# Four of eight pairs with seven products in the down projection of a decoder block

## The chip, the cores and the metric

The kernel runs on one core of a Trainium2 chip. The metric is the device time of one execution in microseconds. The kernel before took 1487.53 us (median of 3 runs, 1486.21 to 1487.73). One further execution was taken with the hardware profiler and took 1486.3 us; every row below comes from that one. The profiler granted TensorE a clock of 0.997 of full speed over it, which is the 2.4 GHz level throughout.

## The reference: what is computed

One block of a decoder for 256 tokens of 2048 channels in float32:

```
h = rmsnorm(x);  z = h @ w_in    # 2048 -> 3072 for three mixers, 512 q, 576 kv, 4 * 2048 gates
y_i = mixer_i(z) @ proj_i                # pooling, convolution, spatial gating, latent attention
x = x + rmsnorm((sum of sigmoid(gate_i) * y_i) @ w_out)
h = rmsnorm(x)
f = square(relu(h @ w_up)) @ w_down      # 2048 -> 8192 -> 2048
x = x + rmsnorm(f)
```

## The kernel before

Every product of float32 matrices is made of three TensorE matmuls, on a high and a low part of each operand (xh·wh, xh·wl, xl·wh). A weight item of 1 MB comes by a DMA on SP's queue into one of three `raw` buffers. ACT rounds a piece of it into `hi` (L102), DVE subtracts that from it into `lo` (L103). `hi` and `lo` have four buffers each, and `w_get` keeps three pieces ahead of TensorE, so that a cast waits until TensorE has read the piece four places before it.

PSUM has eight banks of 512 columns, four of a kind `bank` and four `aux`; a matrix product holds its bank from its first matmul until ACT or DVE has read it. The order of the work is the order in which Python code emits it: generators (`spawn`, `yield`, `tick`) put the small work of norms, rotary embedding and convolution between the pieces of the large products, and a scheduler keeps each engine's order fixed. An instruction that waits therefore holds back all that stands behind it on its engine.

**The start.** The inputs are loaded in pairs of 128 channels together with the weights of q and of kv. The first weights of q come by a DMA that ACT issues (L174) behind one for the gains. Sixteen such steps accumulate `zq` (two banks of 512 columns) and `zkv` (two of 288); the second half of kv, 224 + 64 columns, follows in a loop of its own. When it ends, the statistic of the input norm is ready, and `latent` copies `zq` and `zkv` to SBUF with the scale (L365), takes squares (L369), normalises (L375), transposes (`tp`) and splits into `lat` (L381). TensorE goes on with the convolution's blocks `cva` and `cvg`, which take over the banks of `zkv`. Where a generator needs a product of TensorE, that product stands between those blocks (`rb_ps`, `tp`).

**Norms.** The sum of squares of a row arrives by ACT's accumulator in four parts; `total` adds them, and `rsqrt` takes the power -0.5 on POOL (L263) and refines it on DVE with one Newton step (L265 to L270). The first of these norms over rows is in the middle, between the output projection and the up projection (`first_norm`, `hn_part`); the last one is at the end, in the tail.

**The up and down projections** run in four quarters, q = 0 to 3. A quarter computes 16 blocks of 128 hidden channels (`block_tr`, L223 and L226), keeps them split in `fx`, and multiplies them by its rows of w_down. All of that but the last quarter's second half goes through `eight_sums`: seven calls, for q = 0, 1, 2 with column halves h = 0 and 1, and q = 3 with h = 0. It handles 16 k-blocks as eight pairs of 2 x 2 blocks. A pair listed in `SEVEN` uses a Strassen scheme: seven products of 128x512 into banks M1 to M7, from weights that DVE has combined in place (`first`, `second`, L159 to L163) and activations that `keep_sums` prepared in `sx`. Any other pair uses the eight plain products, into M2, M3, M4 and M8. Eight banks are summed over all pairs; at the end they are added to `acc`, in SBUF. For q = 0 ACT copies them (L1169), for q = 1 to 3 DVE adds them (L1171). `combine` then adds the eight sums to the four results (L1118), once per column half. The last quarter's second half uses plain products, `chunk_nat` for columns c = 2, and a group for each token tile for c = 3.

**The tail.** While that runs, `xr`, the residual kept in DRAM, is loaded back by POOL (L1184), and `combine(0)` runs on DVE with ACT's squares (L1141). Then come `evac_f` for the last columns (L1190), the norm, and `put` (L1213), which multiplies, adds the residual and starts a DMA of 256 KB to the output for each of eight pieces.

Of the kernel before, what the change touches and what calls it, by code (L numbers as in the profile page):

```python
# [15 lines left out]
P = 128  # L16
# [16 lines left out]
QK_SCALE = 192 ** -0.5  # L33
TWO_PI = 6.283185307179586

SEVEN = (1, 3, 5)
SEVEN_G = (1, 3, 5)


# [35 lines left out]
def trunk(ctx: ExitStack, tc: tile.TileContext, t: dict):  # L75
# [90 lines left out]
    def w_emit():  # L166
        if not pending:
            it = next(items, None)
            if it is None:
                return False  # L170
            src, n, step = it
            raw = wp.tile([P, PC], F32, tag="raw", name="raw", bufs=3)
            if step == "first":
                nc.scalar.dma_start(raw[:, :512], src[0][:, :512])  # L174
                nc.sync.dma_start(raw[:, HC:n], src[1])
                nc.sync.dma_start(raw[:, 512:HC], src[0][:, 512:])
                pending.extend((raw[:, o:o + m], None) for o, m in ((0, 512), (HC, 288), (512, 512), (HC + 288, 288)))
# [79 lines left out]
    mhalf = cst.tile([P, NT], F32, name="mhalf")  # L257
    G.memset(mhalf, -0.5)

    def rsqrt(out, var, n):  # L260

        u = w1("nw")[:, :n]
        G.tensor_tensor(out, var, mhalf[:, :n], ALU.pow)  # L263
        if n == 1:
            V.scalar_tensor_tensor(u, out, var, out, ALU.mult, ALU.mult)  # L265
        else:
            V.tensor_tensor(u, out, out, ALU.mult)
            V.tensor_tensor(u, u, var, ALU.mult)
        V.tensor_scalar(u, u, -0.5, 1.5, ALU.mult, ALU.add)
        V.tensor_tensor(out, out, u, ALU.mult)  # L270
# [6 lines left out]
            o += w  # L277

    g_in = small("g_in", KD)
    nc.scalar.dma_start(g_in, t["pre_mix_g"])  # L280
    warm = small("warm", NT)
    A.activation(warm, mhalf, AF.Copy, scale=mhalf[:, :1])
    hx = big.tile([P, KD, NT, S], F32R, tag="A", name="hx")
    xT = big.tile([P, KD, S], F32, tag="B", name="xT")
    ones = cst.tile([P, P], F32, name="ones")
    V.memset(ones, 1.0 / 512)

# [20 lines left out]
    zq = [aux(f"zq{i}") for i in range(NT)]  # L308
    zkv = [[bank(f"zkv{i}{c}") for c in range(2)] for i in range(NT)]
    for k in range(0, KD, 2):  # L310
        nc.sync.dma_start(xT[:, k:k + 2], t["xT"][:, k:k + 2])
        for j in range(k, k + 2):
            if k == 0 or j == k:
                w = [w_get(0), w_get(0)]
            A.activation(hx[:, j, 0], xT[:, j], AF.Copy, scale=g_in[:, j:j + 1])
            V.scalar_tensor_tensor(hx[:, j, 1], xT[:, j], g_in[:, j:j + 1], hx[:, j, 0].bitcast(F32),
                                   ALU.mult, ALU.subtract)
            r = j - k if k else 0
            mm_nat(zq, hx, j, w[0], r * 512, 512, j == 0, j == KD - 1)
# [35 lines left out]
    lat = x16("lat")  # L355
    cqx, ckvx = lat[:, :4], lat[:, 4:]

    def latent(zs, xs, gain, name):

        cn = t4("cn")  # L360
        st = small(f"st_{name}", NT)
        for i in range(NT):
            o = i * 512
            for ps, w in zs[i]:
                A.activation(cn[:, o:o + w], ps[:, :w], AF.Copy, scale=rstd[:, i:i + 1])  # L365
                o += w
# [20 lines left out]
    def spread(out, v):  # L387

        for i in range(NT):
            V.tensor_scalar(out[:, i * P:(i + 1) * P], ident, 0.0, v[:, i:i + 1], ALU.mult, ALU.add)  # L390

    def setup():
        for k in range(KD - 6, KD, 2):
            add_square(k)
# [7 lines left out]
        V.tensor_scalar(ss, ps[:, :NT], 512.0 / D, EPS, ALU.mult, ALU.add)  # L402
        rsqrt(rstd, ss, NT)
        yield 0
        spawn(latent([[(zq[i], 512)] for i in range(NT)], cqx, qg, "cq"))
        yield 0

        posf = small("posf", NT)
# [62 lines left out]
        done.add("kr")  # L471

    spawn(rope_key())
    spawn(latent([[(zkv[i][0], 288), (zkv[i][1], 224)] for i in range(NT)], ckvx, kvg, "ckv"))


    glu = t4("glu").rearrange("p (b s) -> p b s", b=4)
# [467 lines left out]
    def total(parts, n, name):  # L945
# [4 lines left out]

        def rest(beside=None):
            o = small(name)
            v = V.scalar_tensor_tensor(pre, parts[:, n - 1:n], 1.0 / D, pre, ALU.mult, ALU.add)
            if beside:
                with tc.issue_after(v.ins):
                    beside()
            rsqrt(o, pre, 1)
            return o
        return rest

# [126 lines left out]
    def first_hidden(fx):  # L1087
# [17 lines left out]
            yield 1  # L1105
        done.add("u0")

    dr = ctx.enter_context(tc.tile_pool(name="dr", bufs=1, space=bass.MemoryType.DRAM))
    kept = dr.tile([P, NT, D], F32, name="kept")
    xr = mp.tile([P, NT, D], F32, tag="og", name="xr")  # L1110
    sx = mp.tile([P, len(SEVEN), 2, 512], F32R, tag="xg", name="sx")
    fst = [small(f"fst{i}", 4) for i in range(NT)]
    acc = [None, None]

    def combine(h, final):

# [22 lines left out]

    def square_f(i, c, *_):  # L1140
        A.activation(w2("sq"), row_at(i, c), AF.Square, scale=r2sq[i], accum_out=fst[i][:, c:c + 1])  # L1141

    for q in range(NQ):
        fx = big.tile([P, KQ, 2, S], F32R, tag="B", name="fx")
# [22 lines left out]
        def evac(h, b, ps):  # L1167
            if q == 0:
                A.copy(acc[h][:, b], ps[b])  # L1169
            else:  # L1170
                V.tensor_tensor(acc[h][:, b], ps[b], acc[h][:, b], ALU.add)  # L1171

        for h in range(2 if q < NQ - 1 else 1):
            eight_sums(fx, lambda i, o: tuple(sx[:, i, a, o * P:(o + 1) * P] for a in range(2)), SEVEN,
# [33 lines left out]
    rest = [total(fst[i], 4, f"rf{i}") for i in range(NT)]  # L1208
    ws = [w_get(0) for _ in range(4)]

    def put(i, r, c):
# [99 lines left out]
```

## Time and profile before

| what | value |
|---|---|
| median of 3 runs | 1487.53 us |
| profiled execution, whole | 1486.3 us |
| its span, first to last instruction | 1484.6 us |
| PE busy | 1469.7 us, 99% |
| DVE busy | 1171.1 us, 79% |
| ACT busy | 791.5 us, 53% |
| POOL busy | 19.3 us, 1% |
| DMA, 40 slices | 0.3 to 0.8 busy, mean 199 GB/s |

The busy time of an engine is a mean over stages. The chain of waits, followed back from the last instruction, says which engine's work set the end; a list by engine says what that engine waited for and how long. The rows of a timeline begin with the start in microseconds from the span's start and a busy time; what stands in brackets is the idle time of the engine just before the row, and what ended it.

### The profile page before, as it was taken

To read this page: it belongs to the slowest core of one execution; us is meant where nothing else is said; L and a number is where in the kernel's file an instruction comes from. 1 tells how busy PE (TensorE), PEld (TensorE's weight loads), DVE (VectorE), ACT (ScalarE), POOL (GpSimd) and SP (SyncE) were. 2 spreads that over 40 slices of the span, in tenths; PEclk is the share of its full clock that TensorE was granted. 3 is DMA by queue.
4 is the path that set the end of the run, shared out by engine and by line. 5 is a ranking of instruction groups with operands and counts; after the bars stand their busy time and mean duration, and the time that the engine had idled before them with its cause. 6 is when DMAs were issued, how large, how long until landed. Compare 5 with 4: busy or idle time off the path is not lost.

```text
span 1484.6 us, 18697 instructions
## 1 busy us (share of the span) xinstructions
PE 1469.7 (99%) x7213; PEld 1242.1 (84%) x7213; DVE 1171.1 (79%) x1644; ACT 791.5 (53%) x1062; POOL 19.3 (1%) x36
## 2 busy tenths in 40 slices
PE   9999999999999999999999999999999999999997
PEld 8888888888888888888888888888888888888885
DVE  6878788977888888887657877767887779887785
ACT  6655656445554554554444756655544555555552
POOL 0100000000000000000000000000000000000000
PEclk9999999999999999999999999999999999999998
DMA  8555544545645645646756656555566546555573
GB/s 287 206 193 173 182 158 161 198 171 170 226 170 200 225 170 200 225 168 231 284 201 227 253 170 211 216 197 184 172 211 217 184 166 227 204 193 189 167 270 111
DMA packets 57688, 295.75 MB, mean 199 GB/s; under 512 B 5184, under 2 KB 5312, under 8 KB 37120
## 3 DMA queue, kind: packets, MB, share of 16 engines
q1 hardware_dynamic: 55360, 280.41, 53.9%
q0 software_dynamic: 1952, 13.89, 2.5%
q8 instruction: 56, 0.92, 0.2%
q10 hardware_dynamic: 288, 0.27, 0.1%
q14 instruction: 32, 0.26, 0.0%
HBM read 290.36 MB, written 4.19 MB: 198 GB/s over the span
## 4 chain that ended last, share of the span: by engine, by line
PE 96%; DMA 2%; issue 1%; DVE 1%; ACT 0%; POOL 0%; POOLq 0%; DVEq 0%; ACTq 0%
PE up L223 15%; PE sum L814 12%; PE sum L813 12%; PE sum L815 12%; PE up L226 8%; PE yb L212 2%; PE yb L213 2%; PE yb L214 2%; PE zg L212 2%; PE zg L214 2%; PE zg L213 2%; PE o L213 1%; PE o L214 1%; PE o L212 1%; DMA xg<-in_x 1%; PE hd L223 1%
## 5 line engine op out<-in xcount | busy, mean ns | idle before, releaser
L102 ACT CAST hi<-raw 128x1024 fp32r<-128x1024 f32 (+2 forms) x612 | 614.3, 1015 | 453.3 <-PE sum L815 144.8
L103 DVE TENSOR_TENSOR lo<-raw,hi 128x1024 fp32r<-128x1024 f32 (+2 forms) x612 | 708.4, 1175 | 181.3 <-ACT hi L102 173.8
L223 PE MATMUL up<-h,hi 128*128 128x512 f32 x960 | 229.9, 391 | 0.0
L223 PEld LDWEIGHTS up<-h,hi 128*128 128x128 f32 x960 | 176.4, 188 | 34.1
L814 PE MATMUL sum<-lo,fx 128*128 128x512 f32 x343 | 133.4, 389 | 0.0
L813 PE MATMUL sum<-hi,fx 128*128 128x512 f32 x343 | 133.4, 389 | 0.0
L815 PE MATMUL sum<-hi,fx 128*128 128x512 f32 x343 | 133.4, 389 | 0.0
L226 PEld LDWEIGHTS up<-h,lo 128*128 128x128 f32 x960 | 123.1, 191 | 4.7
L226 PE MATMUL up<-h,lo 128*128 128x256 f32 x960 | 124.8, 283 | 0.0
L814 PE MATMUL sum<-lo,hx 128*128 128x512 f32 x312 | 121.4, 389 | 0.0
L815 PE MATMUL sum<-hi,hx 128*128 128x512 f32 x312 | 121.4, 389 | 0.0
L813 PE MATMUL sum<-hi,hx 128*128 128x512 f32 x312 | 121.4, 389 | 0.0
L251 ACT COPY jn<-up 128x256 f32<-128x256 f32 x60 | 22.3, 372 | 122.9 <-PE up L223 122.8
L252 DVE TENSOR_TENSOR u<-up,jn 128x256 f32<-128x256 f32 x60 | 25.4, 423 | 71.5 <-ACT jn L251 71.5
L813 PEld LDWEIGHTS sum<-hi,fx 128*128 128x128 f32 x343 | 64.4, 188 | 13.6
L815 PEld LDWEIGHTS sum<-hi,fx 128*128 128x128 f32 x343 | 64.4, 188 | 13.4
L814 PEld LDWEIGHTS sum<-lo,fx 128*128 128x128 f32 x343 | 64.4, 188 | 13.4
L814 PEld LDWEIGHTS sum<-lo,hx 128*128 128x128 f32 x312 | 58.6, 188 | 12.3
L813 PEld LDWEIGHTS sum<-hi,hx 128*128 128x128 f32 x312 | 58.6, 188 | 12.2
L815 PEld LDWEIGHTS sum<-hi,hx 128*128 128x128 f32 x312 | 58.6, 188 | 12.2
L505 DVE SCALAR_TENSOR_TENSOR cy<-glu,consts,cy 128x253 f32<-128x253 f32 (+15 forms) x120 | 55.2, 462 | 0.6
L212 PE MATMUL zg<-hi,hx 128*128 128x512 f32 x128 | 51.5, 403 | 0.0
(409 smaller groups left out, 2327.8 us busy)
## 6 DMA issues: line engine op xcount, KB each, us to landing
raw<-in_w_g SPq DMA_DIRECT2D x64, 1024.0 KB, 5.4
raw<-in_w_up SPq DMA_DIRECT2D x64, 1024.0 KB, 4.9
raw<-in_w_down SPq DMA_DIRECT2D x64, 1024.0 KB, 5.5
raw<-in_w_out SPq DMA_DIRECT2D x16, 1024.0 KB, 4.9
raw<-in_attn_proj SPq DMA_DIRECT2D x8, 1024.0 KB, 4.9
raw<-in_w_ca SPq DMA_DIRECT2D x4, 1024.0 KB, 4.9
raw<-in_w_cg SPq DMA_DIRECT2D x4, 1024.0 KB, 4.9
raw<-in_w_sv SPq DMA_DIRECT2D x4, 1024.0 KB, 4.8
```

The costliest lines, as they stand in the source:

```text
L102: a = A.copy(hi, src)
L103: return a, V.tensor_tensor(lo, src, hi.bitcast(F32), ALU.subtract)
L212: T.matmul(o, xh, wh, start=first, stop=False)
L213: T.matmul(o, xh, wl, start=False, stop=False)
L214: T.matmul(o, xl, wh, start=False, stop=last)
L223: T.matmul(ps, w[0][:, off:off + P], xs[:, k].rearrange("p a s -> p (a s)"), start=first, stop=last)
L226: T.matmul(ps[:, :S], w[1][:, off:off + P], xs[:, k, 0], start=False, stop=False)
L252: V.tensor_tensor(out, ps[:, :S], r, ALU.add)
L505: V.scalar_tensor_tensor(y, glu[:, b, :S - w], c, y, ALU.mult, ALU.add)
L813: T.matmul(ps[b], xh, wh, start=first, stop=False)
L814: T.matmul(ps[b], xh, wl, start=False, stop=False)
L815: T.matmul(ps[b], xl, wh, start=False, stop=not left[b])
```

## The change

- `SEVEN` goes from (1, 3, 5) to (0, 2, 4, 6): four pairs have seven products, four have eight. `sx` gets four entries, and the first block of the hidden layer keeps sums for pair 0.
- For q = 1 to 3 the eight bank sums are no longer added to `acc` by DVE. ACT copies each bank into a buffer (four into a new `stage`, four into work tiles `e`), and POOL issues a DMA of 256 KB that adds the buffer to `acc`.
- `combine` begins 4 steps later for h = 0 and 6 for h = 1.
- First loads: the first weights of q go on SP's queue as its first item, and the first inputs come in two DMAs, one on ACT's queue and one on SP's.
- `latent` is taken apart: the first 288 columns of `zkv` are copied in `setup`, with `zq`, before the rest.
- The norms over rows take a square root on ACT and a reciprocal on DVE, where POOL's power stood; a square root of a dummy is emitted ahead of the output projection.
- In the tail, the last eight k-blocks of the last token tile are cut: four as before with 512 columns, and four twice with 256 columns, into two new banks `end0` and `end1`, with their own squares and gains; the norm of that tile then adds five parts.

```
-SEVEN = (1, 3, 5)
+SEVEN = (0, 2, 4, 6)
...
             if step == "first":
-                nc.scalar.dma_start(raw[:, :512], src[0][:, :512])
+                nc.sync.dma_start(raw[:, :512], src[0][:, :512])
+                nc.sync.dma_start(xT[:, 1:2], t["xT"][:, 1:2])
...
-        G.tensor_tensor(out, var, mhalf[:, :n], ALU.pow)
+        if root is None:
+            G.tensor_tensor(out, var, mhalf[:, :n], ALU.pow)
+        else:
+            V.reciprocal(out, root)
...
+    nc.scalar.dma_start(xT[:, :1], t["xT"][:, :1])
+    nc.scalar.dma_start(g_in, t["pre_mix_g"])
...
-        spawn(latent([[(zq[i], 512)] for i in range(NT)], cqx, qg, "cq"))
+        spawn(latent([[(zq[i], 0, 512)] for i in range(NT)], cqx, qg, "cq"))
+        half.append(part_of([[(zkv[i][0], 0, 288)] for i in range(NT)]))
...
-    spawn(latent([[(zkv[i][0], 288), (zkv[i][1], 224)] for i in range(NT)], ckvx, kvg, "ckv"))
+    spawn(latent([[(zkv[i][1], 288, 224)] for i in range(NT)], ckvx, kvg, "ckv", half[0]))
...
+            root = small(name + "s")
+            A.activation(root, parts[:, n - 1:n], AF.Sqrt, scale=1.0 / D, bias=pre)
...
-            rsqrt(o, pre, 1)
+            rsqrt(o, var, 1, root)
...
+    stage = mp.tile([P, PC], F32, tag="rg", name="stage", bufs=2)
...
+        yield 6 if h else 4
         add(M2, M1)
...
-                V.tensor_tensor(acc[h][:, b], ps[b], acc[h][:, b], ALU.add)
+                e = stage[:, b * 512:(b + 1) * 512] if b < 4 else w2("e")
+                A.copy(e, ps[b])
+                G.dma_start(acc[h][:, b], e, accum_op=ALU.add)
...
-    tok_group(ps[1], fx, 8, 1, ws, False, True)
-    with tc.issue_after(evac_f(1, 3).ins):
-        put(0, ra, 3)
-    rb = rest[1](lambda: gain_f(1, 3))
+    tok_group(ps[1], fx, 8, 1, ws[:2], False, True)
+    f = row_at(1, 3)
+    V.tensor_tensor(f, ps[1], f, ALU.add)
+    ends = [bank(f"end{h}") for h in range(2)]
+    for h in range(2):
+        for j in range(4):
+            mm_tok(ends[h][:, :S], fx, 12 + j, 1, ws[2 + j // 2], j % 2 * 512 + h * S, S, j == 0, j == 3)
```

Three places where the order of instructions moves are shown below.

Before:

```order
L426 ACT_TABLE_LOAD
L426 ACTIVATE sin<-ang 128x64
L102 CAST hi<-raw 128x1024
L427 ACTIVATE cos<-rnd 128x64
L381 ACTIVATE lat<-tp,consts 128x256 x2
L365 ACTIVATE cn<-zkv_97,rstd 128x224
L369 ACTIVATE sq,st_ckv<-cn 128x512
L381 ACTIVATE lat<-tp,consts 128x256
L365 ACTIVATE cn<-zkv_99,rstd 128x224
L102 CAST hi<-raw 128x1024
```

ACT at the same place with the change:

```order
L438 ACT_TABLE_LOAD
L438 ACTIVATE sin<-ang 128x64
L102 CAST hi<-raw 128x1024
L439 ACTIVATE cos<-rnd 128x64
L102 CAST hi<-raw 128x1024
L390 ACTIVATE lat<-tp,consts 128x256 x2
L102 CAST hi<-raw 128x1024
L369 ACTIVATE cn<-zkv_98,rstd 128x224
L390 ACTIVATE lat<-tp,consts 128x256
L369 ACTIVATE cn<-zkv_100,rstd 128x224
```

The copies of the second kv columns now stand behind two more casts of weights.

POOL in the last quarter; `acc_7439` holds the first column half, and the eight DMAs into it are, in order, for M1 and M7, then M5 and M6, then M2, M4, M3 and M8. Before:

```order
L1080 DMA kept<-xr 128x4096
L263 TENSOR_TENSOR r_7048<-r20p,mhalf 128x1
L263 TENSOR_TENSOR r_7171<-r21p,mhalf 128x1
L1184 DMA xr<-kept 128x4096
L263 TENSOR_TENSOR rf_12353<-rf0p,mhalf 128x1
L263 TENSOR_TENSOR rf_12396<-rf1p,mhalf 128x1
```

POOL with the change:

```order
L1199 DMA acc_7440<-stage 128x512 x4
L1199 DMA acc_7440<-e 128x512 x4
L1199 DMA acc_7439<-stage 128x512 x2
L1212 DMA xr<-kept 128x4096
L1199 DMA acc_7439<-stage 128x512 x2
L1199 DMA acc_7439<-e 128x512 x4
```

The load of the residual now stands between the second and the third of the last eight adding DMAs.

DVE at the combination of the first column half, beside the end of the last `eight_sums` and the columns c = 2. Before:

```order
L1118 TENSOR_TENSOR acc_7417<-acc_7417 128x512
L103 TENSOR_TENSOR lo<-raw,hi 128x1024
L1171 TENSOR_TENSOR acc_7417<-sum,acc_7417 128x512 x2
L103 TENSOR_TENSOR lo<-raw,hi 128x1024
L1118 TENSOR_TENSOR acc_7417<-acc_7417 128x512
L1180 SCALAR_TENSOR_TENSOR acc_7417<-acc_7417,r2sq_6699,rg 128x512
L1118 TENSOR_TENSOR acc_7417<-acc_7417 128x512
L103 TENSOR_TENSOR lo<-raw,hi 128x1024
L1118 TENSOR_TENSOR acc_7417<-acc_7417 128x512 x3
```

DVE with the change:

```order
L163 TENSOR_TENSOR raw<-raw 128x512
L103 TENSOR_TENSOR lo<-raw,hi 128x1024 x9
L1135 TENSOR_TENSOR acc_7439<-acc_7439 128x512 x2
L103 TENSOR_TENSOR lo<-raw,hi 128x1024
L1135 TENSOR_TENSOR acc_7439<-acc_7439 128x512
L1208 SCALAR_TENSOR_TENSOR acc_7439<-acc_7439,r2sq_6707,rg 128x512
L1135 TENSOR_TENSOR acc_7439<-acc_7439 128x512
L103 TENSOR_TENSOR lo<-raw,hi 128x1024
L1135 TENSOR_TENSOR acc_7439<-acc_7439 128x512 x3
```

The first two additions of the combination now stand behind nine `lo` (four of the last two pairs, five of the columns c = 2) and ahead of the sixth `lo` of c = 2.

## Rows read from the trace of the kernel before

**Rows 1.** The page: busy time of TensorE, and the chain's shares by engine.
```profile
PE 1469.7 (99%) x7213; PEld 1242.1 (84%) x7213; DVE 1171.1 (79%) x1644; ACT 791.5 (53%) x1062; POOL 19.3 (1%) x36
PE 96%; DMA 2%; issue 1%; DVE 1%; ACT 0%; POOL 0%; POOLq 0%; DVEq 0%; ACTq 0%
```

**Rows 2.** Waits of TensorE: line, releaser, us in total, times, longest.
```profile
PE zq L212 <- ACT hi L102: 1.6, 1, 1.6
PE cva L223 <- ACT cn L365: 1.1, 1, 1.1
PE tph L1019 <- DVE hn L1014: 0.2, 1, 0.2
```

**Rows 3.** Timeline of TensorE in `eight_sums`, first and last of 45 matmuls: start, us.
```profile
1239.84 0.39 PE L813 MATMUL sum<-hi,fx 128*128 128x512 f32 x1
...
1249.84 0.39 PE L815 MATMUL sum<-hi,fx 128*128 128x512 f32 x1
```

**Rows 4.** Timeline of the start, ACT and TensorE.
```profile
6.55 0.62 ACT L102 CAST hi<-raw 128x512 fp32r<-128x512 f32 x1 [1.30 <-DMA raw<-in_w_q]
...
13.57 1.62 ACT L102 CAST hi<-raw 128x1024 fp32r<-128x1024 f32 x2 [0.66 <-DMA raw<-in_w_q]
...
16.04 0.39 PE L212 MATMUL zq<-hi,hx 128*128 128x512 f32 x1
```

**Rows 5.** Windows, 0 to 25 us; last three columns: PE clock, DMA share, GB/s.
```profile
0.00:25.00 25.00, 22.26 (x118) 19.98 (x119) 15.79 (x27) 17.00 (x30) 1.19 (x8) 1.00 0.91 316
```

**Rows 6.** Timelines of ACT, DVE and TensorE around the latents, 56 to 71 us.
```profile
57.87 1.28 ACT L426 ACT_TABLE_LOAD   x1
59.74 0.87 DVE L375 TENSOR_SCALAR cn<-cn,r_cq 128x512 f32<-128x512 f32 x2
62.89 0.45 ACT L365 ACTIVATE cn<-zkv,rstd 128x224 f32<-128x224 f32 x1 [0.90 <-DVE krt L458]
63.65 2.10 PE L223 MATMUL cvg<-hx,hi 128*128 128x512 f32 x8
69.74 1.05 ACT L102 CAST hi<-raw 128x1024 fp32r<-128x1024 f32 x1 [2.09 <-PE cvg L223]
```

**Rows 7.** Timelines of POOL and DVE at the first norm over rows.
```profile
773.39 0.57 POOL L263 TENSOR_TENSOR r<-r10p,mhalf 128x1 f32<-128x1 f32 x1 [12.77 <-DVE r10p L953]
783.78 1.42 DVE L1014 SCALAR_TENSOR_TENSOR hn<-og,r,xg 128x512 f32<-128x512 f32 x2
```

**Rows 8.** DMA issues: times, KB each, us from issue to landing.
```profile
xr<-kept POOLq DMA_DIRECT2D x1, 2048.0 KB, 12.5
poolw<-in_pool_w POOLq DMA_DIRECT2D x1, 256.0 KB, 3.0
```

**Rows 9.** Timeline of ACT beside the load of the residual.
```profile
1429.82 1.05 ACT L102 CAST hi<-raw 128x1024 fp32r<-128x1024 f32 x1 [3.60 <-DMA raw<-in_w_down]
```

**Rows 10.** Lines by shape, 1050 to 1485 us: busy us, mean ns, idle before and releasers.
```profile
L103 DVE TENSOR_TENSOR lo<-raw,hi 128x1024 fp32r<-128x1024 f32 x171 | 206.1, 1221 | 33.0 <-ACT hi L102 29.9
L102 ACT CAST hi<-raw 128x1024 fp32r<-128x1024 f32 x171 | 178.7, 1054 | 108.6 <-PE sum L815 53.6 <-DVE raw L159 24.2 <-DMA raw<-in_w_down 11.8
L1171 DVE TENSOR_TENSOR acc<-sum,acc 128x512 f32<-128x512 f32 x40 | 26.2, 682 | 3.0 <-PE sum L815 3.0
L1118 DVE TENSOR_TENSOR acc<-acc 128x512 f32<-128x512 f32 x16 | 10.5, 683 | 0.0
```

**Rows 11.** Line L1169, ACT's copies of banks: ns min/median/max.
```profile
L1169 ACT COPY acc<-sum x16: 574/585/602, 899.4 to 955.6; 128x512 f32<-128x512 f32 x16
```

**Rows 12.** Timelines of the tail, and sixteen 256-column matmuls of the chain.
```profile
806.56 1.91 PE up L226 x16
...
1468.69 0.69 DVE L1190 TENSOR_TENSOR acc<-dn,acc 128x512 f32<-128x512 f32 x1 [3.13 <-PE dn L214]
1475.98 0.98 POOL L263 TENSOR_TENSOR rf<-rf1p,mhalf 128x1 f32<-128x1 f32 x1 [4.47 <-DVE rf1p L953]
1477.63 2.74 DVE L1213 SCALAR_TENSOR_TENSOR acc<-acc,rf,xr 128x512 f32<-128x512 f32 x4
```

More of the change, by code (lines that the diff above doesn't have):

```diff
@@ L258, in trunk, with rsqrt @@
     G.memset(mhalf, -0.5)
-    def rsqrt(out, var, n):
+    def rsqrt(out, var, n, root=None):
         u = w1("nw")[:, :n]
-        G.tensor_tensor(out, var, mhalf[:, :n], ALU.pow)
+        if root is None:
+            G.tensor_tensor(out, var, mhalf[:, :n], ALU.pow)
+        else:
+            V.reciprocal(out, root)
         if n == 1:
@@ L279, in trunk @@
     g_in = small("g_in", KD)
-    nc.scalar.dma_start(g_in, t["pre_mix_g"])
     warm = small("warm", NT)
-    A.activation(warm, mhalf, AF.Copy, scale=mhalf[:, :1])
     hx = big.tile([P, KD, NT, S], F32R, tag="A", name="hx")
     xT = big.tile([P, KD, S], F32, tag="B", name="xT")
+    nc.scalar.dma_start(xT[:, :1], t["xT"][:, :1])
+    nc.scalar.dma_start(g_in, t["pre_mix_g"])
+    A.activation(warm, mhalf, AF.Copy, scale=mhalf[:, :1])
     ones = cst.tile([P, P], F32, name="ones")
@@ L310, in trunk @@
     for k in range(0, KD, 2):
-        nc.sync.dma_start(xT[:, k:k + 2], t["xT"][:, k:k + 2])
+        if k:
+            nc.sync.dma_start(xT[:, k:k + 2], t["xT"][:, k:k + 2])
         for j in range(k, k + 2):
@@ L356, in trunk, with part_of, latent @@
     cqx, ckvx = lat[:, :4], lat[:, 4:]
-    def latent(zs, xs, gain, name):
-        cn = t4("cn")
-        st = small(f"st_{name}", NT)
[L362 to L366, printed above, removed]
+    def part_of(zs, cn=None):
+        cn = cn or t4("cn")
+        for i in range(NT):
+            for ps, o, w in zs[i]:
+                A.activation(cn[:, i * 512 + o:i * 512 + o + w], ps[:, :w], AF.Copy, scale=rstd[:, i:i + 1])
+        return cn
+    def latent(zs, xs, gain, name, cn=None):
+        st = small(f"st_{name}", NT)
+        cn = part_of(zs, cn)
         yield 0
@@ L390, in spread @@
             V.tensor_scalar(out[:, i * P:(i + 1) * P], ident, 0.0, v[:, i:i + 1], ALU.mult, ALU.add)
+    half = []
     def setup():
@@ L952, in rest @@
             o = small(name)
-            v = V.scalar_tensor_tensor(pre, parts[:, n - 1:n], 1.0 / D, pre, ALU.mult, ALU.add)
+            root = small(name + "s")
+            A.activation(root, parts[:, n - 1:n], AF.Sqrt, scale=1.0 / D, bias=pre)
+            var = small(name + "v")
+            v = V.scalar_tensor_tensor(var, parts[:, n - 1:n], 1.0 / D, pre, ALU.mult, ALU.add)
             if beside:
@@ L964, in trunk @@
     st = [small(f"ost{i}", 4) for i in range(NT)]
+    A.activation(warm, ident[:, :NT], AF.Sqrt)
     r1 = [None] * NT
@@ L1111, in trunk @@
     sx = mp.tile([P, len(SEVEN), 2, 512], F32R, tag="xg", name="sx")
-    fst = [small(f"fst{i}", 4) for i in range(NT)]
+    fst = [small(f"fst{i}", 4 + i) for i in range(NT)]
     acc = [None, None]
@@ L1141, in square_f, with half_f @@
         A.activation(w2("sq"), row_at(i, c), AF.Square, scale=r2sq[i], accum_out=fst[i][:, c:c + 1])
+    def half_f(ps, h):
+        s = slice(h * S, (h + 1) * S)
+        f = row_at(1, 3)[:, s]
+        e = V.tensor_tensor(f, ps[:, :S], f, ALU.add)
+        A.activation(w1("sq"), f, AF.Square, scale=r2sq[1], accum_out=fst[1][:, 3 + h:4 + h])
+        return e, f
     for q in range(NQ):
@@ L1207, in trunk @@
             mm_nat(ps, fx, k + j, w, j * 512, 512, k + j == 0, False)
-    rest = [total(fst[i], 4, f"rf{i}") for i in range(NT)]
+    rest0 = total(fst[0], 4, "rf0")
     ws = [w_get(0) for _ in range(4)]
@@ L1216, in trunk, with gain_h @@
     evac_f(0, 3)
-    ra = rest[0](lambda: gain_f(0, 3))
+    ra = rest0(lambda: gain_f(0, 3))
     for c in range(3):
         put(0, ra, c)
-    tok_group(ps[1], fx, 8, 1, ws, False, True)
-    with tc.issue_after(evac_f(1, 3).ins):
-        put(0, ra, 3)
-    rb = rest[1](lambda: gain_f(1, 3))
+    tok_group(ps[1], fx, 8, 1, ws[:2], False, True)
[5 more added lines that the diff above has]
+            mm_tok(ends[h][:, :S], fx, 12 + j, 1, ws[2 + j // 2], j % 2 * 512 + h * S, S, j == 0, j == 3)
+    e, f0 = half_f(ends[0], 0)
+    with tc.issue_after(e.ins):
+        put(0, ra, 3)
+    rest1 = total(fst[1], 5, "rf1")
+    def gain_h(h, f):
+        V.scalar_tensor_tensor(f, f, r2sq[1], pog[:, 3 * 512 + h * S:3 * 512 + (h + 1) * S], ALU.mult, ALU.mult)
+    gain_h(0, f0)
+    e, f1 = half_f(ends[1], 1)
+    with tc.issue_after(e.ins):
+        gain_h(1, f1)
+    rb = rest1()
     for c in range(4):
```

## The prediction

> **What bounds the kernel.** I read the page's busy times first, then the chain, then TensorE's waits. The reader is to see that TensorE is busy for 99% of the span and makes up 96% of the chain [rows 1], at the high clock level throughout, and that only three of its waits bear on this change: 1.6 us at the start, 1.1 us at the convolution's first block, 0.2 us at the first norm over rows [rows 2]. So an edit can pay in three ways only: fewer TensorE columns, one of those waits gone, or a shorter start or tail. It can cost wherever something comes late for TensorE. After that I read, from the order of each engine, where the change moves instructions. It does so in five places: start, 50 to 65 us, the first norm, the down projection, and the tail. I price each from the timeline of that place.
>
> **The fourth pair: -4.8.** A call of `eight_sums` goes from 3 x 7 + 5 x 8 = 61 products to 4 x 7 + 4 x 8 = 60. Seven calls make 7 products of 3 matmuls, 21 matmuls of 512 columns. From 1239.84 to 1249.84 lie 45 matmuls, 44 steps in 10.00 us, 0.2273 us each [rows 3]. 21 x 0.2273 = 4.77. DVE must keep up with the extra combination: a pair of seven costs it 1.22 + 0.68 + 1.22 + 1.22 of `lo` and 1.22 + 0.69 + 0.69 on `raw`, 6.94; a pair of eight costs 2 x 1.22 = 2.44 [rows 10] (the half-width `raw` steps, 0.69, cost what the additions of that width do). With the eight additions of banks, 0.68 each [rows 10], a call cost DVE 38.5 of 61 x 3 x 0.2273 = 41.6 us; now it costs 4 x 6.94 + 4 x 2.44 = 37.5 of 40.9. The additions go to ACT as copies of 0.585 [rows 11], 40 of them, 23 us; ACT has 108.6 us of idle time before its casts in this stretch [rows 10], so it hides them. If that cover failed, TensorE would lose up to 0.6 per copy at a call's end, where banks are taken over; the copies come a piece later than the bank's last product, as before, so I put nothing. The extra activation sums of pair 0 lie beside the up blocks, where DVE is not full. I also put nothing for the q = 0 to 2 accumulating DMAs: nobody reads their target before the next quarter.
>
> **The late combination: +2.1.** This is the term I know least. In the last quarter all eight bank sums of h = 0 must land in `acc` before DVE can combine them. POOL's queue is in order: two adding DMAs, then the 2 MB load of the residual, then the other six. That load waits for the last reader of `sx`, pair 6, at a time I call t0; 24 matmuls of pair 7 follow, so the columns c = 2 begin at t0 + 5.45. The load took 12.5 us from issue to landing beside the weight loads [rows 8], and is issued about 0.7 after t0, so it lands at t0 + 13.2. If the six additions follow in series at x us each, M2 lands at t0 + 13.2 + 3x, M4 at + 4x, M3 at + 5x, M8 at + 6x. DVE's order puts the first two additions (2 x 0.68 [rows 10]) ahead of the sixth `lo` of c = 2. A piece there is 12 matmuls, 2.73 us; the sixth is needed at t0 + 5.45 + 13.87 = t0 + 19.3. Less 1.22 for the `lo` and 1.36 for the additions, M2 must be there by t0 + 16.75. Counted in the same way through ACT's square ahead of the seventh cast, M4 must be there by about t0 + 18.8, and M3 and M8 by t0 + 23 and + 25. The trace of before has no adding DMA. From below, a plain share of the load's own pace, 12.5 / 8 = 1.56: M2 at + 17.9, a stall of 1.1. From above, three times that, since an addition moves its operands twice in and once out: 4.7, with M8 at + 41, a stall of 16. A lone 256 KB load on POOL's queue took 3.0 from issue to landing [rows 8], part of which overlaps when several are queued. I take 1.9, nearest to the lower row: DMA is not full here, though casts already waited up to 3.60 for weights beside that load [rows 9]. Then M2 is there at + 18.9, a stall of 2.1, and M4 to M8 fit behind it.
>
> For such a DMA on POOL's queue the Trainium skill has a price (DMA: Bandwidth & Descriptors, section Anatomy of one DMA, SWDGE path): about 2.0 us fixed plus the bytes at 436 GB/s. An estimate from it is 2.6 us for 256 KB; paid in series this would make the stall 4.8 and the whole sum +1.7 instead of -1.0. The 2 MB load's 12.5 us lies above its 6.8, and no run here yet shows an adding one.
>
> **The start: -0.4** (-1.5 to +0.2). The first cast waits 1.30 for weights [rows 4] that ACT issues as its second DMA; now they come first on SP's queue, and the first product may start up to 1.5 earlier. But TensorE soon meets the third step: its cast waited 0.66 for its DMA and ends its first `hi` at 13.57 + 1.05 = 14.62, the `lo` takes 1.22, with the handover to 15.88, and TensorE needs it for its second matmul at 16.27 [rows 4, 10]. So 0.39 of slack is all that an earlier start can use, since the bytes ahead of that weight are the same and DMA is 0.91 busy at 316 GB/s [rows 5].
>
> **The early copies: +1.5** (-1.1 to +2.0). The wait of 1.10 [rows 2] is for a bank of `zkv`, and its copy is now early, so it goes. What is late next: the norm of the q latent, whose DVE step stands at 59.74 [rows 6]. Its inputs are no earlier (the early copies even stand before those of `zq`), so TensorE, 1.1 ahead, waits at the products that stand behind that norm. And `cvg` needs the bank of a 224-column copy. Before, that copy ran at 62.89, ahead of the cast behind it; `cvg` began at 63.65 [rows 6]. Now two more casts stand before it, and the second needs a buffer that TensorE frees only with the last wide products of `cva`, at about 63.5: ring waits of this kind exist, 2.09 at 69.74 [rows 6]. Cast 0.95 and copy 0.45 behind it, with handover, put `cvg` at 65.15 instead of 63.65. If the ring turns out free, the full 1.1 is won.
>
> **Roots on ACT: +0.6** (0 to +1.4). At the first norm POOL's power of 0.57 [rows 7] goes and a table load of 1.28 [rows 6], a root of about 0.3 and a reciprocal of about 0.15 come; the dummy root does not help, since its place on ACT is early and other tables follow. For the first token tile products cover it. For the second the chain was tight: `hn` began at 783.78 [rows 7], and TensorE waited 0.2 [rows 2]; 1.28 + 0.3 + 0.15 - 0.57 = 1.2 more, of which I let half come through, since the square ahead of the root moves too.
>
> A table switch has a price in the Trainium skill as well (ScalarE: Activation LUTs, section What ACT_TABLE_LOAD costs): 1283 ns and a drain of 1380 ns. The trace agrees with the first at 1.28; by the second this term would be an estimated 1.4 higher, the sum +0.4.
>
> **The tail: 0** (-0.6 to +0.6). 24 matmuls of 256 columns at 1.91 / 16 = 0.119 [rows 12] replace 12 of 512: 24 x 0.119 - 12 x 0.2273 = +0.14. The power of 0.98 at 1475.98 [rows 12] leaves the last chain for a root and a reciprocal, and the last square is half as long. Against that, DVE's order puts three writes of the first tile, one half's addition, and a fourth write ahead of the last half's addition, which then ends 7.2 after the first tile's products, where it was 6.2 after them (the addition at 1468.69 is the mark). The last four writes begin 9.0 after it in both, as at 1477.63 [rows 12].
>
> **The sum.** -4.8 + 2.1 - 0.4 + 1.5 + 0.6 + 0 = -1.0, from 1486.3 of the profiled execution to 1485.3. The median of the runs is 1.23 above that execution (1487.53), so I predict 1486.5.
>
> **The rivals.** First, the adding DMAs keep the plain pace or overlap, and the early copies or the start give half of what they promise: -4.8 + 0.5 + 0.3 and nothing else lost, -4: 1483.5. For it: only six of the 40 adding DMAs have a deadline within the same quarter, and the page's other waits are nearly nothing [rows 2]; against it: the order at the three places above. Second, slower: the adding DMAs queue behind the residual at 2.9 us or more. Then M4 comes at t0 + 24.8, 6 late; ACT's square and DVE's additions stand in their queues ahead of casts and `lo`, and TensorE stands still. From x = 2.9 on the sum is about +3 or more; at 3.3, M4 is 7.6 late, +4.5: 1492. For it: the lone load of 3.0 [rows 8] and casts that wait for weights already [rows 9]. Against it: a lone load's time is mostly latency, which a queue hides. Third, `cvg` does not wait: the early-copy term is -1.1 instead of +1.5, the sum -3.6, 1483.9; that needs the buffer ring to be ahead at one place where 2.09 was waited before a little later.
>
> **How the numbers follow.** The forecast has 0.43, its own range 1484 to 1489; the first rival 0.30; slower 0.17; the third 0.10. A measurement of this kernel tells from no change about 0.2%, which is 3 us. Of the forecast 0.08 falls faster and 0.02 slower; of the first rival 0.28 faster; of the second 0.16 slower and 0.01 within; of the third 0.06 faster. Faster 0.08 + 0.28 + 0.06 = 0.42, slower 0.02 + 0.16 = 0.18, the rest 0.40. The range goes from 1482.5, a little past the first rival, to 1492, the second at x = 3.3; the far end of x, over 1500, is left out.
>
> **What would show it.** Right: 21 fewer matmuls in `eight_sums` at an unchanged pitch; a wait of TensorE for `lo` or `hi` in the columns c = 2 of the last quarter, 1 to 3 us, released by a chain that ends in an adding DMA; `cvg` at 64.5 or later counted from the end of the input products as before; a table load just ahead of the first root. Wrong: no wait of TensorE in c = 2 (then x is small or the additions overlap), a first product 1.5 earlier that keeps its lead beyond 25 us, a DVE that lags in `eight_sums`, or waits of ACT for the `stage` buffers in q = 1 and 2.

## The result and the profile after

The changed kernel takes 1498.23 us (median of 4, 1497.17 to 1499.51) against 1487.19 for the kernel before: ratio 1.0075, 95% interval 1.0058 to 1.0093, so 11.0 us slower. That is outside the range 1482.5 to 1492.0, and the wrong way: the prediction, 1486.5, lay 1.0 us under the kernel before. The span of the profiled execution went from 1484.6 to 1495.6 us.

TensorE's waits of the kernel after (line, releaser, us in total, times, longest) answer to [rows 2]:

```profile
PE dn L214 <- DVE lo L103: 6.3, 1, 6.3
PE up L227 <- DVE lo L103: 4.7, 1, 4.7
PE rb_ps L446 <- DVE rep L399: 1.5, 1, 1.5
PE sum L826 <- DVE lo L103: 1.4, 2, 0.8
...
PE zu L215 <- DVE h L103: 0.6, 1, 0.6
```

There are two large new waits, both for a weight's `lo` on DVE. Read one step back, in DVE's own waits:

```profile
DVE acc L1135 <- DMA acc<-e: 20.0, 2, 11.5
```

DVE stands twice, 20.0 us together, before an addition of `combine` (L1135) whose operand an adding DMA has not yet landed. Every `lo` behind it in DVE's queue stands too. The first place is the start of the last quarter, DVE's timeline:

```profile
1297.51 1.23 DVE L103 TENSOR_TENSOR lo<-raw,hi 128x1024 fp32r<-128x1024 f32 x1 [2.60 <-ACT hi L102]
1307.22 2.14 DVE L1135 TENSOR_TENSOR acc<-acc 128x512 f32<-128x512 f32 x3 [8.49 <-DMA acc<-e]
1309.28 2.35 DVE L103 TENSOR_TENSOR lo<-raw,hi 128x1024 fp32r<-128x1024 f32 x2
```

The second is in the columns c = 2, DVE:

```profile
1438.75 1.23 DVE L103 TENSOR_TENSOR lo<-raw,hi 128x1024 fp32r<-128x1024 f32 x1 [1.18 <-ACT hi L102]
1451.49 1.42 DVE L1135 TENSOR_TENSOR acc<-acc 128x512 f32<-128x512 f32 x2 [11.51 <-DMA acc<-e]
1452.82 1.22 DVE L103 TENSOR_TENSOR lo<-raw,hi 128x1024 fp32r<-128x1024 f32 x1
```

and TensorE there:

```profile
1447.39 0.39 PE L213 MATMUL dn<-hi,fx 128*128 128x512 f32 x1
1454.10 0.80 PE L214 MATMUL dn<-lo,fx 128*128 128x512 f32 x1 [6.32 <-DVE lo L103]
1454.69 0.63 PE L215 MATMUL dn<-hi,fx 128*128 128x512 f32 x1
1455.12 0.63 PE L213 MATMUL dn<-hi,fx 128*128 128x512 f32 x1
```

After the wait the steps from one matmul to the next are 0.43 us, where they were 0.227 in [rows 3]. The windows of TensorE (us, busy and count, granted clock, DMA share, GB/s) say why; the second group cuts one microsecond out of the first place:

```profile
1304.00:1308.00 4.00, 1.82 (x12) 1.00 1.13 205
1308.00:1312.00 4.00, 1.45 (x6) 0.81 0.65 104
1312.00:1316.00 4.00, 4.00 (x16) 0.77 0.58 238
1316.00:1320.00 4.00, 4.00 (x27) 1.00 0.66 252
...
1311.00:1312.00 1.00, 1.00 (x6) 0.50 0.80 98
...
1450.00:1455.00 5.00, 0.90 (x2) 0.54 0.78 141
1455.00:1460.00 5.00, 5.00 (x19) 0.78 0.58 210
```

In both places the clock fell to the lower level (0.50 and 0.54 of full speed, 1.2 of 2.4 GHz): in the second during the wait of 6.3 us, in the first as the wait of 4.7 us ended. It came back to 1.00 some 3 us after the work did. So a wait cost more than the wait.

A ledger by marks shows it. Each row is the start of TensorE's first matmul of a part, before and after, and the change since the row above:

| mark | before | after | after - before | step |
|---|---|---|---|---|
| first up block, q = 0 | 804.58 | 804.03 | -0.55 | -0.55 |
| first `sum`, q = 0 | 872.29 | 871.74 | -0.55 | 0 |
| first up block, q = 1 | 955.41 | 953.55 | -1.86 | -1.31 |
| first up block, q = 2 | 1127.60 | 1125.56 | -2.04 | -0.18 |
| first up block, q = 3 | 1299.78 | 1297.33 | -2.45 | -0.41 |
| first `sum`, q = 3 | 1388.85 | 1392.88 | +4.03 | +6.48 |
| first `dn` | 1430.41 | 1433.79 | +3.38 | -0.65 |
| first tile's last addition (DVE) | 1468.69 | 1480.12 | +11.43 | +8.05 |
| end of the span | 1484.6 | 1495.6 | +11.0 | -0.4 |

The pair gains what it should where nothing disturbs it: -1.31 over the two calls of q = 0 (2 x 0.68 expected), -0.65 over the last call. Quarters 1 and 2 gain only 0.18 and 0.41 of 1.36. The two places of DVE's waits lose 6.48 and 8.05, of which 4.7 and 6.3 are the waits themselves and the rest is mostly the low clock.

How late are the adding DMAs? Rows of DMA issues, one issue each, give KB and the us from issue to landing: the first of quarter 2's second call, then, from the last quarter, the residual and the M5 behind it:

```profile
acc<-stage POOLq DMA_DIRECT2D x1, 256.0 KB, 7.0
...
xr<-kept POOLq DMA_DIRECT2D x1, 2048.0 KB, 15.9
...
acc<-stage POOLq DMA_DIRECT2D x1, 256.0 KB, 19.5
```

### The profile page after: what moved, and what is told of

Read it like the earlier page. It is cut to its first block, busy times and chain, and to the rows that moved or that the text cites. A ratio compares the mean times of both kernels' runs of the same rounds, so it can differ in the third digit from the quotient of the medians.

```text
span 1495.6 us, 18898 instructions
## 1 busy us (share of the span) xinstructions
PE 1469.1 (98%) x7204; PEld 1242.2 (83%) x7204; DVE 1180.9 (79%) x1668; ACT 822.8 (55%) x1131; POOL 49.2 (3%) x70
## 4 chain that ended last, share of the span: by engine, by line
PE 71%; issue 22%; DMA 3%; POOL 2%; DVE 2%; ACT 0%; DVEq 0%; POOLq 0%; ACTq 0%
PE sum L826 8%; PE sum L825 8%; PE sum L827 8%; PE up L224 7%; PE up L227 4%; PE yb L213 2%; PE yb L214 2%; PE yb L215 2%; PE zg L215 2%; PE zg L213 2%; PE zg L214 2%; POOL acc L1199 2%; PE o L214 1%; DMA acc<-e 1%; PE o L215 1%
## 5 line engine op out<-in xcount | busy, mean ns | idle before, releaser
L103 DVE TENSOR_TENSOR lo<-raw,hi 128x1024 fp32r<-128x1024 f32 (+2 forms) x626 | 720.2, 1171 | 177.8 <-ACT hi L102 172.0
L102 ACT CAST hi<-raw 128x1024 fp32r<-128x1024 f32 (+2 forms) x626 | 623.8, 1010 | 421.7 <-PE sum L827 100.1
L826 PE MATMUL sum<-lo,fx 128*128 128x512 f32 x308 | 120.2, 390 | 1.4 <-DVE lo L103 1.4
L825 PE MATMUL sum<-hi,fx 128*128 128x512 f32 x308 | 120.0, 390 | 0.0
L827 PE MATMUL sum<-hi,fx 128*128 128x512 f32 x308 | 119.9, 389 | 0.0
L826 PEld LDWEIGHTS sum<-lo,fx 128*128 128x128 f32 x308 | 57.8, 188 | 14.0 <-DVE lo L103 2.1
L826 PEld LDWEIGHTS sum<-lo,hx 128*128 128x128 f32 x312 | 58.6, 188 | 12.2
L825 PEld LDWEIGHTS sum<-hi,hx 128*128 128x128 f32 x312 | 58.6, 188 | 12.2
L825 PEld LDWEIGHTS sum<-hi,fx 128*128 128x128 f32 x308 | 57.8, 188 | 12.5 <-ACT hi L102 0.2
L827 PEld LDWEIGHTS sum<-hi,fx 128*128 128x128 f32 x308 | 57.8, 188 | 11.9
L159 DVE TENSOR_TENSOR raw<-raw 128x1024 f32<-128x1024 f32 x46 | 56.1, 1219 | 0.0
```

What stands on the lines that cost most here:

```text
L102: a = A.copy(hi, src)
L103: return a, V.tensor_tensor(lo, src, hi.bitcast(F32), ALU.subtract)
L159: V.tensor_tensor(b4[:, :, 0], b4[:, 1], b4[:, :, 0], ALU.subtract)
L825: T.matmul(ps[b], xh, wh, start=first, stop=False)
L826: T.matmul(ps[b], xh, wl, start=False, stop=False)
L827: T.matmul(ps[b], xl, wh, start=False, stop=not left[b])
```

## The experiments

**Theory.** The additions of `combine` stand in DVE's fixed order ahead of the landing of the adding DMAs. **Rivals.** The DMAs are too much traffic for the weight loads; DVE cannot carry the fourth pair; the early edits cost the time; it is the residual's load on the same queue.

**late_both.** The additions pinned behind the `lo` last issued (`issue_after` keeps an instruction behind another in its engine's order), and for h = 1 begun later:

```
-            V.tensor_tensor(acc[h][:, a], acc[h][:, a], acc[h][:, b], ALU.add)
+            with tc.issue_after(newest[1]):
+                V.tensor_tensor(acc[h][:, a], acc[h][:, a], acc[h][:, b], ALU.add)
-        yield 6 if h else 4
+        yield 14 if h else 4
```

> The changed kernel with the additions of combine tied behind the weight subtraction last issued on DVE, and begun 14 steps later for h = 1 (4 for h = 0 as in the change). The adding DMAs and the order of POOL's queue stay. Theory (DVE's in-order additions wait for adding DMAs that have not landed; TensorE then stands still and comes back at the lower clock level): both stalls go, 6.5 us in the up blocks of the last quarter and 8.05 us in the columns c = 2, so 1498.2 - 14.5 = 1483.7, no wait of TensorE over 1 us in either place. Rival (the DMAs themselves are too much traffic beside the weight loads, and the waits come back for weights): stays above 1490.

Measured 1491.16 (ratio to before 1.0028, 1.0018 to 1.0037): 7 us back, half of what was expected. The wait in the up blocks is gone. In the columns c = 2 the additions now stand behind twelve `lo`, and DVE still waited 6.5 there (TensorE 4.1, in two waits):

```profile
1448.06 1.42 DVE L1136 TENSOR_TENSOR acc<-acc 128x512 f32<-128x512 f32 x2 [6.50 <-DMA acc<-e]
```

The profiled execution is the fastest of the ten, at 1488.4. The median lies where the rival put it, above 1490, and this run alone does not refute the rival: what TensorE waited for is still DVE's additions, but M2 took 23.9 us to land here, and between 1420 and 1460 us ACT's casts waited 10.7 us for weights, 1.8 in the change. No run tries the later start of h = 1 without the pinning.

**xr_on_act.** `G.dma_start(xr, kept)` becomes `nc.scalar.dma_start(xr, kept)`.

> The changed kernel with one thing else: the load of the residual is issued by ACT, on ACT's queue, not between the adding DMAs on POOL's. Theory that the load ahead of them on the same queue makes them late: M2 lands some 12 us after its issue as in the earlier quarters, about 15.5 us after the last reader of sx, before DVE needs it at 16.75, and the stall in c = 2 goes: 1498.2 - 8 = 1490.2; the one in the up blocks stays at 4.7 us of waiting. Rival (the adding DMAs share the sixteen engines with 2 MB in any queue, and the place of the additions is what matters): M2 is still late by 3 us or more, and the time is 1494 or above.

Measured 1505.36 (1.0125, 1.011 to 1.014): worse, and the theory's number is missed by 15. TensorE waited 13.1 in c = 2. Two things show. M2 landed 17.4 after its issue, where it took 12.4 in quarter 2 of the same run, so the residual slows the adding DMAs from another queue as well. And the order moved: with the residual out of POOL's queue, the scheduler put four additions behind six `lo`, where the first two had stood behind nine, and DVE waited longer for M2:

```profile
1452.07 2.87 DVE L1135 TENSOR_TENSOR acc<-acc 128x512 f32<-128x512 f32 x4 [17.48 <-DMA acc<-e]
```

**pair_only.** The kernel before with `SEVEN = (0, 2, 4, 6)`.

> The kernel before with only the table of pairs changed to (0, 2, 4, 6); the bank sums stay with DVE, and nothing else is moved. Theory (the fourth pair gains its 4.8 us, and DVE, at 43.0 us of work in a call of 40.9, falls behind by some 2 us a call, which the three pieces of look-ahead take up in part): 1482.5 to 1487, with TensorE waiting for lo in the later calls. Rival (DVE cannot keep up, which would be the reason for moving the sums): 1490 or more, waits for lo of 2 us in each of five calls.

Measured 1484.68 (0.9983, 0.9973 to 0.9992): inside the theory's range, 2.6 of the 4.8 gained. By marks the quarters 1 and 2 gain 0.32 and 0.41 of 1.36, so DVE's extra work costs about 1 us a quarter, and not 2 us a call. DVE keeps up but for that.

**rest_only.** The change with `SEVEN = (1, 3, 5)`, the bank sums on DVE, no delay of `combine`.

> The changed kernel with three pairs (1, 3, 5), the bank sums back on DVE and the combination not delayed; the first loads, early latent copies, roots on ACT and the cut tail stay. Theory (the ledger by marks: -0.55 us up to the down projection and -0.4 at the end): 1487.2 - 1.0 = 1486.2. Rival (some of the 11 us come from these edits): above 1488.

Measured 1485.89 (0.9992, 0.9982 to 1.0001), 1.4 under the 1487.25 of before in the same session, not clearly different from it. No sign that any of the 11 us come from these edits.

**mixed.** The last quarter's sums on DVE, the others by DMA, h = 1 combined late:

```
+            elif q == NQ - 1:
+                V.tensor_tensor(acc[h][:, b], ps[b], acc[h][:, b], ALU.add)
...
-        yield 6 if h else 4
+        if h:
+            yield 14
```

(and the pinning of late_both for h = 1).

> The changed kernel with the bank sums of the last quarter added by DVE as before the change, and the h = 1 combination begun 14 steps later and tied behind the weight subtraction last issued; the quarters 1 and 2 keep the adding DMAs. Theory (the loss is the two places where DVE's additions wait for adding DMAs; the rest of the DMAs cost only the 2.1 us that the weight loads lose): both stalls and their time at the lower clock go, 1498.2 - 14.5 = 1483.7. Rival (the adding DMAs cost more than that through the weight loads): above 1487, with waits of TensorE for lo or hi spread over quarters 1 and 2.

Measured 1483.12 (0.9969, 0.9957 to 0.998): the theory's number. No wait of TensorE over 1.5 us is left.

**rest_pair.** All bank sums by `V.tensor_tensor`, as before the change, with everything else of it but the delay of `combine`.

> The changed kernel with all bank sums added by DVE and the combination not delayed: four pairs, first loads, early copies, roots on ACT and cut tail, without the adding DMAs. Theory (the parts add up): 1487.25 - 2.57 (the pairs alone) - 1.36 (the rest alone) = 1483.3. Rival (DVE, over its time in the later calls, loses what the rest gains): 1485 or more.

Measured 1483.2 (0.9973, 0.9962 to 0.9984), as added up. With the adding DMAs out altogether the change is 4 us faster than before; so the DMAs and the delayed combination, as the change has them, cost 15 us.

**pool_adds.** `G.tensor_tensor(acc, e, acc)` instead of the adding DMA.

> The changed kernel with the addition done by POOL's own arithmetic on the copies in SBUF instead of by a DMA. Theory (what costs is the landing time of the DMA, not that DVE is relieved or that the combination stands early): an addition on POOL of under 2 us each is done within some 4 us of its copy, both stalls go, the weight loads keep their 5.5 us, and DVE is relieved: 1498.2 - 14.5 - 2.1 = 1481.6. Rival (POOL's arithmetic hinders DVE): DVE's subtractions of 128x1024 rise above 1.22 us beside the additions and TensorE waits for lo; 1485 or more.

Measured 1501.3 (1.0091, 1.0076 to 1.0106): the rival. Lines by shape, last 450 us (busy us, mean ns, idle before):

```profile
L103 DVE TENSOR_TENSOR lo<-raw,hi 128x1024 fp32r<-128x1024 f32 x174 | 236.2, 1381 | 22.1 <-ACT hi L102 19.8
L1199 POOL TENSOR_TENSOR acc<-stage,acc 128x512 f32<-128x512 f32 x20 | 39.7, 2002 | 554.8 <-ACT stage L1198 554.7
L1135 DVE TENSOR_TENSOR acc<-acc 128x512 f32<-128x512 f32 x16 | 14.8, 947 | 1.5 <-POOL acc L1199 1.2
```

An addition takes POOL 2.0 us, and DVE's subtraction rose from 1221 ns [rows 10] (1222 in the change) to 1381 on the mean of all 174, though POOL was busy for only 79 of those 450 us. Of the theory one half held: DVE's wait before the additions of `combine` shrank from 20.0 us to 1.5. TensorE instead waits for `hi` and `lo` in `eight_sums`:

```profile
PE sum L826 <- DVE lo L103: 6.0, 2, 3.0
PE sum L825 <- ACT hi L102: 3.9, 2, 2.0
```

**plain_copy.** `G.dma_start(acc[h][:, b], e)` without `accum_op`: the same DMAs copy, and the sums of quarters 1 to 3 are left out.

> The changed kernel with DMAs that copy the bank over the target and do not add (the sums of quarters 1 to 3 are left out). Theory (the addition in the DMA is what makes it slow): the first of a call lands 4 us or less after its issue and the next ones 1.5 us apart, where the adding ones take 6.8 to 7.0 and are 2.5 apart; the wait in the up blocks goes. Rival (it is the queue's share of the engines beside weight loads with rows of 4 KB and more, against its own of 2 KB): landing times stay within 1 us of those of the adding DMAs, and so do both stalls.

One run: 1489.86. The first copy of the call that took 7.0 when adding landed after

```profile
acc<-stage POOLq DMA_DIRECT2D x1, 256.0 KB, 2.5
```

and M2 after 8.8 where the adding one took 12.2. The waits shrink to 1.3 in the up blocks and 3.7 in c = 2, and do not go: between theory and rival. So the addition accounts for 4.5 us at the head of a call and 3.4 for M2; the rest is the queue beside other loads, and it is late even for plain copies. The pages also show what an addition takes of the 16 DMA engines. The rows of POOL's queue (packets, MB, share of the engines' span) are, without the 40 DMAs (rest_pair), with them copying, and with them adding (the change):

```profile
q0 software_dynamic: 1952, 13.89, 2.5%
q0 software_dynamic: 5152, 24.38, 4.3%
q0 software_dynamic: 7712, 24.38, 6.3%
```

For the same bytes the adding DMAs are 5760 packets where the copies are 3200, and take 3.8% of the engines' time where the copies take 1.8%.

**xr_last.** The residual tied behind the last adding DMA, on POOL's queue:

```
+    with tc.issue_after(sums_by[0]):
+        G.dma_start(xr, kept)
```

> The changed kernel with the load of the residual tied behind the last adding DMA on POOL's queue; the additions of combine stand where the change puts them. Theory (in the columns c = 2 what is late is the six adding DMAs that share the queue or the engines with those 2 MB): M2 lands about 12 us after its issue as in quarter 2, some 15.5 after the last reader of sx, where DVE needs it at 16.75; the wait of 6.3 goes, the one of 4.7 in the up blocks stays: 1498.2 - 8.05 = 1490.2. Rival (the additions stand too early for adding DMAs in any case): a wait of 3 us or more is left in c = 2, 1494 or above.

Measured 1497.0 (1.0069, 1.0053 to 1.0086): the rival's number, with a wait of 4.8 in c = 2. Yet M2 landed 12.4 after its issue, as the theory said. DVE's timeline:

```profile
1434.48 1.23 DVE L103 TENSOR_TENSOR lo<-raw,hi 128x1024 fp32r<-128x1024 f32 x1 [3.96 <-ACT hi L102]
1442.97 2.14 DVE L1136 TENSOR_TENSOR acc<-acc 128x512 f32<-128x512 f32 x3 [7.26 <-DMA acc<-e]
```

The order explains it, DVE of xr_last ahead of the additions:

```
L163 TENSOR_TENSOR raw<-raw 128x512
L103 TENSOR_TENSOR lo<-raw,hi 128x1024 x7
L1136 TENSOR_TENSOR acc_7439<-acc_7439 128x512 x3
```

Seven `lo`, where the change has nine. The scheduler moved the additions forward by two pieces, 5.5 us of TensorE's time, presumably because it took the sums to be ready earlier; its estimates are not on record. What the earlier DMAs gained was lost again by the order, so this run alone could not tell theory from rival.

**late_and_last.** Both: additions pinned as in late_both, residual last as in xr_last.

> The changed kernel with both: the additions of combine pinned behind twelve weight subtractions instead of nine in the last quarter (and 14 steps late for h = 1), and the load of the residual behind the last adding DMA. All sums of quarters 1 to 3 stay with the DMAs. Theory (what costs is that DVE's fixed order has the additions ahead of the landing; in xr_last M2 landed 12.4 us after its issue but the additions had moved two subtractions forward): M2 lands some 9 us before the pinned place wants it, no wait of TensorE over 1 us in c = 2 or c = 3, 1498.2 - 14.5 = 1483.7. Rival (six adding DMAs cannot be hidden this near to the end): a wait of 2 us or more is left and the time is 1488 or above, as in late_both (1491.2).

Measured 1482.63 (0.997, 0.9961 to 0.998). DVE runs from its twelfth `lo` into the additions without a wait:

```profile
1439.92 1.22 DVE L103 TENSOR_TENSOR lo<-raw,hi 128x1024 fp32r<-128x1024 f32 x1 [1.50 <-ACT hi L102]
1441.06 1.41 DVE L1137 TENSOR_TENSOR acc<-acc 128x512 f32<-128x512 f32 x2
1442.64 1.22 DVE L103 TENSOR_TENSOR lo<-raw,hi 128x1024 fp32r<-128x1024 f32 x1 [0.17 <-ACT hi L102]
```

M2 landed 14.0 after its issue at 1425.38, at 1439.4, only 1.7 ahead and not 9. No wait of TensorE over 1.5 us is left. All forty adding DMAs are still there; only the order on DVE and on POOL's queue has changed, and 15.6 us are back. This shows the theory. It took both edits: the pinning alone left 1491.16, the moved residual alone 1497.0.

**four_in_one.** One adding DMA of 1 MB for M1, M7, M5 and M6, with rows of 8 KB:

```
+                if b >= 4:
+                    G.dma_start(acc[h][:, b], e, accum_op=ALU.add)
+                elif b == M6:
+                    G.dma_start(acc[h][:, :4], stage.rearrange("p (b n) -> p b n", b=4), accum_op=ALU.add)
```

> The changed kernel with one adding DMA of 1 MB for the banks M1, M7, M5 and M6 (rows of 8 KB instead of 2 KB), issued when the last of them is copied; the other four stay as they are. Theory (beside weight loads with rows of 4 KB and more the queues take turns row by row, so short rows get a small share): the 1 MB lands within 9 us of its issue in quarter 2, where the fourth of the single DMAs landed 12.1 after its own, M2 right behind it, and TensorE waits less than 4.7 in the up blocks. Rival (an addition has its own pace by bytes, about 2.6 us for 256 KB): 10.4 us or more for the 1 MB, M2 13 us or later, and a wait of 5 us or more.

One run: 1500.09. The 1 MB landed in 10.6, M2 in 15.1, TensorE waited 4.8 in the up blocks, in two waits. That is the rival's side in both landing times, and the wait lies between the two forecasts: longer rows do not help. It is no proof of a pace by bytes, since one 256 KB takes 7.0 and four together 10.6, which looks like a long latency and some 1.2 per 256 KB behind it. The runs do not separate the two.

**half_dma.** As mixed, but only the four banks that end first go by DMA; M2, M4, M3, M8 are added by DVE:

```
+            elif q == NQ - 1 or b >= 4:
```

> The kernel called mixed, with only the four banks that end first (M1, M7, M5, M6) copied and added by DMA in quarters 1 and 2; M2, M4, M3 and M8 are added by DVE. Theory (each half costs in proportion: the eight adding DMAs of a call make the weight loads late, eight additions on DVE make the subtractions late): 0.5 to 1.0 us under both mixed and rest_pair, 1482.3. Rival (either cost has a threshold, and neither is reached): 1481.5; or the four DMAs cost as much as eight: 1483.2.

Measured 1481.06 (0.9963, 0.995 to 0.9976): the lowest of all, 5.7 us under before in its session, and near the rival without a cost on either side. Its interval overlaps those of mixed, rest_pair and late_and_last, so the lead rests on the marks. By these the quarters 1 and 2 gain 1.17 and 1.20 of 1.36. TensorE's waits are those of the start and the norms:

```profile
PE rb_ps L446 <- DVE rep L399: 1.5, 1, 1.5
PE idle L295 <- DVE ones L291: 1.1, 1, 1.1
PE zq L213 <- ACT hx L321: 0.9, 1, 0.9
PE zu L215 <- DVE h L103: 0.6, 1, 0.6
```

## Why the prediction was wrong, by its steps

**"Nobody reads their target before the next quarter": failed, worth 6.5.** True (for q = 1 and 2; q = 0 has no such DMA), and no cover: `combine(1)` is spawned at the start of the last quarter, and its first addition stands behind seven `lo` in DVE's order, four of `eight_sums` and three of the new up blocks. DVE came to it when M2 had still 8.5 us to go: M2 landed at 1307.2, 9.9 us into the next quarter. The prediction read DVE's order at one combination and not at the other. The 6.5 are 4.7 of waiting and the lower clock behind it.

**The late combination, +2.1: mechanism right, measured 8.05.** The forecast had M2 at t0 + 18.9. With t0 = 1433.79 - 5.45 = 1428.3 it was there at t0 + 23.1. The deadline was right: 23.1 less 16.75 is 6.35, and TensorE waited 6.32. Of the 4.2 that M2 was late, 3.2 are the load of the residual, which landed at t0 + 16.4 instead of 13.2. The other 1.0 is the pace: M5 landed 4.2 after the residual, not 1.9, and M6 and M2 behind it some 1.25 apart. The rest of the 8.05 is mostly the lower clock, which the sum did not have at all. The second rival (adding DMAs behind the residual) named this mechanism; its 1492 was too low, since it too had one place of two and no lower clock.

**The weight loads: put at nothing, measured about 2.** The quarters 1 and 2 lost 1.2 and 0.9, nearly all of it in one wait of TensorE for a `lo` in each quarter's second call. In quarter 2 its cast on ACT had waited for the weight:

```profile
1269.16 2.00 ACT L102 CAST hi<-raw 128x1024 fp32r<-128x1024 f32 x2 [2.06 <-DMA raw<-in_w_down]
```

That 1 MB took 10.9 us from issue to landing beside the adding DMAs, and 7.0 at the same place of plain_copy. The runs with eight adding DMAs a call lose 0.5 to 1.9 a quarter, half_dma with four 0.2, and plain_copy, with eight copying ones, 0.05. So the copies on ACT do cost nothing, as the prediction had it; the adding DMAs do not. And rest_pair, with no DMA, loses 1.0 too, through DVE's additions, so in these quarters the change exchanged one cost for another.

**The fourth pair, -4.8: right** where undisturbed, as the ledger shows; with what the weight loads took it came to -2.55.

**The start, -0.4: measured -0.82** at the end of the inputs. Across the runs with these edits the mark of the first `hd` lies 0.85 earlier to 0.32 later than in the trace of before, so the size is not resolved.

**The early copies, +1.5: wrong, about +0.2.** ACT, and TensorE's `cvg`:

```profile
63.00 2.09 PE L224 MATMUL cvg<-hx,hi 128*128 128x512 f32 x8
...
63.06 1.05 ACT L102 CAST hi<-raw 128x1024 fp32r<-128x1024 f32 x1 [1.94 <-PE cva L224]
64.02 0.44 ACT L369 ACTIVATE cn<-zkv,rstd 128x224 f32<-128x224 f32 x1
```

The cast did wait for `cva`, and the copy came after `cvg` had begun: `cvg` cannot have taken that bank, `zkv_98`, as the section on the change has it. Presumably it took one that the early copies had freed. The third rival (`cvg` does not wait) was right on that, but not on its 1.1 gained, since TensorE waited 1.5 at `rb_ps` instead.

**The roots, +0.6: measured +0.2** (from -0.78 at the first `zu` to -0.55 at the first up block). One table load served both roots:

```profile
772.01 1.28 ACT L966 ACT_TABLE_LOAD   x1
773.31 0.30 ACT L966 ACTIVATE r10s<-ost,r10p 128x1 f32<-128x1 f32 x1
...
778.42 0.30 ACT L966 ACTIVATE r11s<-ost,r11p 128x1 f32<-128x1 f32 x1
```

The first root begins 1.30 after the load began; the second, `r11s`, has no load ahead of it. Of the drain that the Trainium skill adds (ScalarE: Activation LUTs, section What ACT_TABLE_LOAD costs), nothing shows behind the load here.

**The tail, 0: right.** The last four writes begin at 1489.11, 8.99 after the first tile's addition, where it was 8.94; the -0.4 at the end lies behind them, in the last output DMAs.

**The sum.** Measured by marks: -2.55 for the pairs with the weight loads, +6.48 and +8.05 for the two places, -0.55 for all before the up projection, -0.4 at the end; together +11.0, where -1.0 was forecast.

## What to carry to other kernels

An operation moved to a DMA is free only if every reader stands behind its landing in the reader's own queue: look up each reader in the order of its engine, all of them, and count from the landing, not from the issue. Where a scheduler sets that order, a moved transfer may pull the readers forward and give little or nothing back; pin the readers first, then move the transfer. Where two engines share a load that either can carry nearly alone, try half on each before all on one.

## What was not expected of the hardware

- A 256 KB DMA that adds to SBUF took 7.0 us at the head of a call, a copy of the same bytes on the same queue 2.5. The 40 adding DMAs took 5760 packets and 3.8% of the DMA engines' time, as copies 3200 and 1.8%.
- POOL's addition of 128x512 took 2.0 us and DVE's subtractions rose beside it from 1222 to 1381 ns on the mean.
- After waits of 4.7 and 6.3 us TensorE came back at the lower level; each place lost another 1.7 us beyond its wait, most of it at that level.
